# The opening of a two-layer encoder in a new written order, with the shift carried as a column

## The chip, the cores and the metric

The kernel runs on one core of a Trainium2 chip. The metric is the device time of one execution in microseconds. A core has TensorE (PE, matrix products), VectorE (DVE), ScalarE (ACT), GpSimd (POOL) and SyncE (SP, which here issues the DMAs). Each engine takes its instructions in one order and waits on semaphores for the others. Operands lie in SBUF, and TensorE writes its products to PSUM.

## The reference, cut to what matters

Two sequences, a prompt of 256 rows and a sample of 512 rows, go through a trunk of two layers. Layer 0 mixes with a two-way mLSTM of four heads, layer 1 with windowed attention, and each is followed by a convolutional feed-forward block. What the change touches is the front of layer 0:

```python
mod = silu(c) @ adaln_w[0] + adaln_b[0]          # c: one vector per sequence
sh1, sc1, g1, sh2, sc2, g2 = split(mod, 6)
h = rmsnorm(x, norm_g[0, 0]) * (1 + sc1) + sh1    # per sequence
proj = h @ w_in                                   # q, k, v, o and 16 gate columns
b = cumsum(log_sigmoid(f_gate)); m = running max of (i_gate - b) ...   # per head, both directions
```

Everything is float32. A product of two float32 matrices is built from three passes: each operand is split into a high half (`whi`, `hh`), rounded by ScalarE to the format that TensorE takes at full rate, and a low half (`wlo`, `hl`), the rest, by a subtraction on VectorE. Then high x high, high x low and low x high are added up in PSUM.

## The kernel before

Activations lie transposed: 1024 features as eight chunks (`KC`) of 128 partitions, and 768 columns, of which 0 to 255 are the prompt and 256 to 767 the sample. `RANGES` cuts them into the sample's two halves and the prompt (range 2). `hh` and `hl` hold the high and low halves of the normed input for all 768 columns.

*Norm.* `Norm` (L87 to L140) squares each chunk on ScalarE (L108), adds the squares up on GpSimd (L112, or on the engine given as `adds`), sums over partitions with products against a constant (two columns per 128 rows), takes the power -1/2 on GpSimd (L131), and broadcasts the result over the partitions by TensorE (`pr`). Then the `apply` function given to it scales the input. `stages()` is a generator: one call for the sums, one for the broadcast, one to apply.

*The opening* (L572 to L671) is written in an order by hand for TensorE, ScalarE and VectorE (`manual_schedule`). Its three items are the gates' weights and the two halves of head 0's query weights. It starts the sample's products before the adaLN shift is known. With x the normed input times its gain, (x + shift) W = xW + shift W, so the sample's item is accumulated from the unshifted input, and shift W is added as a bias: `bias(i, z)` multiplies the shift's two halves (`sh`, two columns) by each weight chunk into a spare corner of a PSUM bank, `biased(i)` copies the two columns out and adds them (L651, L652), and ScalarE adds the bias to the whole bank in place (L653). The prompt's items are computed from its shifted input. `shifted` then writes the shifted halves of the prompt and, between the items, of the sample, which all later products read. For the sample, every other chunk goes through ScalarE with a helper tile `hs` from which the shift is taken off again (L554, L556, L563).

The order on TensorE: sample range 0 and 1 items, shift products, prompt items interleaved with shift products. The `adaln` vectors of groups 1 (scale) and 0 (shift) are products of the conditioning vector with eight row tiles each (`vector`, L379 to L408).

*After it*, still in layer 0 but left to the planner, stand the gates' functions and scans. ScalarE computes the logarithm of the sigmoid (L765 to L767), VectorE sums it up along time in both directions (L773, L775), subtracts (L776), and takes running maxima (L779, L780). The maxima `M` go to DRAM (L784) and come back broadcast over partitions (L800). GpSimd adds the masks (L802). Then head 0: its key weights are split (L236 high, L237 low), four products of 24 passes give the keys (`gemmT`, two halves by two sequences), and `keep` evicts them in two halves (queries times 1/16, L239 and L240; keys unscaled, L236 and L237). Six tiles of values follow (`gemmN`, 24 passes each). Scores, exponentials of the masks (L864 to L868) and the weighted sums (L908 to L930) come next, and the same for heads 1 to 3.

*Filling.* Two generators, `adaln_v` (VectorE, layer 1, L472) and `adaln_g` (TensorE, layer 0), compute the rest of the adaLN vectors in small steps that the heads call. They fetch rows of 512 KB through the same five `raw` buffers as the weights. `issue_after` puts the first of `adaln_v` behind the last scan.

*The planner.* Outside the written stretches the order on each engine comes from the tile framework's list scheduler, which takes the instructions by priority (the order of the program) whenever its own model of time says that an engine is free. It can also put such instructions between those of a written stretch. SP and GpSimd are always ordered by it. PSUM has four banks under the name `ps` and four under `pa`; split weights have three buffers each for `whi` and `wlo`.

Of the kernel before, what the change touches and what calls it, by code (L numbers as in the profile page):

```python
# [145 lines left out]
class Net:  # L146
# [232 lines left out]
    def vector(self, pool, grp, rows):  # L379
# [3 lines left out]
        self.spare = ps = self.ps()  # L383
        for k in range(KC):
            for g in range(4):
                self.mm(
                    ps[32 * g : 32 * g + 32, :256], self.silc[:, k, :], rows[k][:, g * 256 : (g + 1) * 256],
                    k == 0, k == KC - 1,
                )
# [130 lines left out]

    def scaled(self, x, pr, rng):
# [4 lines left out]
    def unshifted(self, x, pr, rng):  # L526

        nc = self.nc
        c0, c1, q = rng
        for c in range(KC + 1):  # L530
            if c < KC:
                if pr is not None:
                    nc.vector.tensor_tensor(x(c), x(c), pr, ALU.mult)
                nc.scalar.activation(self.hh[:, c, c0:c1], x(c), AF.Copy, scale=self.gain[0][0][:, c, q : q + 1])
            if c:
                nc.vector.scalar_tensor_tensor(  # L536
                    self.hl[:, c - 1, c0:c1], x(c - 1), self.gain[0][0][:, c - 1, q : q + 1],
                    self.hh[:, c - 1, c0:c1].bitcast(F32), ALU.mult, ALU.subtract,
                )
        return ()  # L540

    def shifted(self, pool, xt, rng, less=None):

# [4 lines left out]
        sub = [None] * KC  # L548
        for c in range(KC + 1):
            if c < KC:  # L550
                gain, shift = self.gain[0][0][:, c, q : q + 1], self.mod[0][:, c, q : q + 1]
                hi = self.hh[:, c, c0:c1]
                if less is not None and c % 2:
                    nc.scalar.activation(hi, x(c), AF.Identity, bias=shift, scale=gain)  # L554
                    sub[c] = pool.tile([P, c1 - c0], F32, tag="E", name=self.nm("hs"), bufs=2)
                    nc.scalar.activation(sub[c], hi.bitcast(F32), AF.Identity, bias=less[:, c : c + 1])  # L556
                else:
                    nc.vector.tensor_scalar(x(c), x(c), gain, shift, ALU.mult, ALU.add)
                    nc.scalar.copy(hi, x(c))
            if c:  # L560
                hi, lo = self.hh[:, c - 1, c0:c1], self.hl[:, c - 1, c0:c1]
                if sub[c - 1] is not None:
                    self.behind_opening = nc.vector.scalar_tensor_tensor(  # L563
# [1166 lines left out]
```

## Time and profile before

| | us |
|---|---|
| median of 3 runs | 1902.51 |
| lowest, highest | 1899.25, 1902.64 |
| span of the profiled execution | 1900.1 |
| median less that span | 2.4 |
| TensorE busy in it | 1812.0 (95%) |
| VectorE, ScalarE, GpSimd busy | 1413.8, 920.9, 491.0 |
| mean granted TensorE clock | 0.983 |

The profiled execution's own time is its span with whatever lies before the first and after the last instruction. Only the span is recorded for it, and the runs' times are near it. Lines from the trace read: start, length, engine, line of the kernel, operation, output `<-` inputs, partitions x elements, how many; in brackets the idle time of the engine before it and what ended that. In a table of stretches each engine has its busy microseconds and its count of instructions; `PEclk` is the share of full speed that TensorE was granted. In a list of waits the numbers are the total, the count and the longest. In a list of groups they are the total busy time and the mean nanoseconds of one.

### The profile page before, as it was taken

How to read it: one execution, taken by the hardware profiler on the slowest of the kernel's cores; microseconds unless marked ns; L12 is line 12 of the kernel's file. 1: busy time of each engine (PE TensorE's matmuls, PEld its weight loads, DVE VectorE, ACT ScalarE, POOL GpSimd, SP SyncE). 2: the span in 40 equal slices, each digit the busy share in tenths (PEclk: the TensorE clock that was granted, in tenths of full speed). 3: DMA queues.
4: the chain of work that ended last, by engine and by line, in shares of the span. 5: the costliest groups of instructions: out<-in, count | busy, mean ns of one | idle time of the engine just before them, and what ended most of it. 6: DMA issues, size and time to landing. Idle time of an engine off the chain costs nothing.

```text
span 1900.1 us, 29288 instructions
## 1 busy us (share of the span) xinstructions
PE 1812.0 (95%) x11354; PEld 1672.5 (88%) x11354; DVE 1413.8 (74%) x2310; ACT 920.9 (48%) x1849; POOL 491.0 (26%) x395
## 2 busy tenths in 40 slices
PE   7889999999999999999999999989989999999997
PEld 5787887888998999999999988879979999999996
DVE  4664776687589877777777768875998777777777
ACT  4633434343456444444444466773564444444443
POOL 3001000022013433333332303330133333333322
PEclk9888999999999999999999999999999999999998
DMA  8243655456412222222222321212222222222211
GB/s 321 66 141 113 210 166 165 153 167 199 144 55 89 67 67 67 67 67 67 67 67 79 112 81 48 84 58 90 78 78 77 68 67 67 67 67 67 67 34 67
DMA packets 64246, 184.49 MB, mean 97 GB/s; under 512 B 6167, under 2 KB 23831, under 8 KB 64108
## 3 DMA queue, kind: packets, MB, share of 16 engines
q1 hardware_dynamic: 64108, 182.63, 29.6%
q8 instruction: 89, 1.46, 0.3%
q14 instruction: 49, 0.40, 0.1%
HBM read 176.17 MB, written 6.43 MB: 96 GB/s over the span
## 4 chain that ended last, share of the span: by engine, by line
PE 76%; DVE 11%; issue 5%; ACT 4%; DMA 2%; POOL 2%; SPq 0%; POOLq 0%; ACTq 0%; DVEq 0%
PE pa L230 23%; PE ps L230 23%; PE ps L1252 10%; PE ps L1253 9%; PE ps L1254 9%; DVE wlo L237 2%; DMA bt<-brow 1%; DVE slab L690 1%; ACT t L1078 1%; DVE t L1069 1%; POOL nt L112 1%; DVE slab L1479 1%; DVE zl L1210 1%; DVE slab L1478 0%; DVE slab L237 0%
## 5 line engine op out<-in xcount | busy, mean ns | idle before, releaser
L236 ACT CAST whi<-raw 128x1024 fp32r<-128x1024 f32 x237 | 248.7, 1049 | 401.1 <-PE pa L230 200.3
L237 DVE TENSOR_TENSOR wlo<-raw,whi 128x1024 fp32r<-128x1024 f32 x237 | 330.7, 1395 | 113.5 <-ACT whi L236 112.8
L230 PE MATMUL pa<-slab,whi 128*128 128x256 f32 (+1 forms) x1472 | 344.8, 331 | 4.4 <-DVE slab L690 4.2
L230 PEld LDWEIGHTS pa<-slab,whi 128*128 128x128 f32 x1472 | 250.9, 188 | 31.4 <-DVE slab L690 5.8
L690 DVE SCALAR_TENSOR_TENSOR slab<-pa,mod,slab 128x256 f32<-128x256 f32 (+1 forms) x368 | 207.8, 592 | 67.5 <-PE pa L230 66.9
L230 PE MATMUL ps<-zh,whi 128*128 128x256 f32 (+2 forms) x688 | 233.6, 340 | 4.4 <-ACT whi L236 2.6
L230 PE MATMUL pa<-slab,wlo 128*128 128x256 f32 (+1 forms) x736 | 234.0, 330 | 0.0
L230 PE MATMUL ps<-zh,wlo 128*128 128x256 f32 (+2 forms) x688 | 228.6, 335 | 4.3 <-DVE wlo L237 4.3
L230 PE MATMUL ps<-zl,whi 128*128 128x256 f32 (+2 forms) x688 | 229.0, 334 | 1.6 <-DVE zl L536 0.9
L1252 PE MATMUL ps<-zh,whi 128*128 128x384 f32 x504 | 171.2, 340 | 14.3 <-ACT ps L1307 13.1
L1253 PE MATMUL ps<-zl,whi 128*128 128x384 f32 x504 | 169.8, 337 | 1.7 <-DVE zl L1210 1.7
L1254 PE MATMUL ps<-zh,wlo 128*128 128x384 f32 x504 | 169.0, 335 | 0.0
L230 PEld LDWEIGHTS pa<-slab,wlo 128*128 128x128 f32 x736 | 138.3, 188 | 13.0 <-DVE wlo L237 0.9
L230 PEld LDWEIGHTS ps<-zh,whi 128*128 128x128 f32 x688 | 132.7, 193 | 18.0 <-ACT whi L236 3.2
L230 PEld LDWEIGHTS ps<-zh,wlo 128*128 128x128 f32 x688 | 132.4, 192 | 15.1 <-DVE wlo L237 5.1
L230 PEld LDWEIGHTS ps<-zl,whi 128*128 128x128 f32 x688 | 132.5, 193 | 11.2 <-DVE zl L536 1.3
L1505 POOL TENSOR_TENSOR slab<-slab 128x772 f32<-128x772 f32 x44 | 83.3, 1893 | 206.7 <-DVE slab L1479 193.9
L1283 POOL TENSOR_TENSOR raw<-raw,raw 128x512 f32<-128x512 f32 x40 | 52.1, 1303 | 294.1 <-DVE wlo L237 244.1
L1478 DVE SCALAR_TENSOR_TENSOR slab<-slab,cstt,slab 128x771 f32<-128x771 f32 x88 | 105.3, 1199 | 26.9 <-ACT slab L1476 26.9
L1479 DVE SCALAR_TENSOR_TENSOR slab<-slab,cstt,slab 128x771 f32<-128x771 f32 x88 | 119.7, 1360 | 0.8
L472 DVE SCALAR_TENSOR_TENSOR ada<-raw,silc,ada 128x1024 f32<-128x1024 f32 x84 | 114.0, 1387 | 6.5 <-DMA raw<-in_adaln_w_dram 6.3
L1252 PEld LDWEIGHTS ps<-zh,whi 128*128 128x128 f32 x504 | 94.7, 188 | 22.2 <-ACT ps L1307 18.2
(309 smaller groups left out, 4182.4 us busy)
## 6 DMA issues: line engine op xcount, KB each, us to landing
raw<-in_w_dram SPq DMA_DIRECT2D x208, 512.0 KB, 3.7
raw<-in_adaln_w_dram SPq DMA_DIRECT2D x84, 512.0 KB, 4.4
slab<-in_x_dram SPq DMA_DIRECT2D x12, 512.0 KB, 7.6
slab<-in_adaln_w_dram SPq DMA_DIRECT2D x12, 512.0 KB, 10.9
slab<-mrows SPq DMA_DIRECT2D x8, 384.0 KB, 5.7
xs<-slab SPq DMA_DIRECT2D x6, 512.0 KB, 2.9
bt<-brow SPq DMA_DIRECT2D x16, 192.0 KB, 3.2
slab<-xs SPq DMA_DIRECT2D x6, 512.0 KB, 6.7
```

Source lines behind the costliest of these rows:

```text
L230: self.last_mm = self.nc.tensor.matmul(out, lhsT, rhs, start=start, stop=stop)
L236: nc.scalar.copy(hi, src)
L237: return nc.vector.tensor_tensor(lo, src, hi.bitcast(F32), ALU.subtract)
L472: stt(acc[:, s], row, w, acc[:, s], ALU.mult, ALU.add)
L690: self.nc.vector.scalar_tensor_tensor(x, o, self.mod[l][:, gc + c, q : q + 1], x, ALU.mult, ALU.add)
L1252: mm(o, wh[:, k], hi[k], start=start and k == 0, stop=False, skip_group_check=True)
L1253: mm(o, wh[:, k], lo[k], start=False, stop=False, skip_group_check=True)
L1254: mm(o, wl[:, k], hi[k], start=False, stop=k == 3, skip_group_check=True)
L1283: tt(q[0], q[2], q[0], ALU.subtract)
L1478: stt(y[:, 1:], u[:, :-1], w(0), y[:, 1:], ALU.mult, ALU.add)
L1479: stt(y[:, :-1], u[:, 1:], w(2), y[:, :-1], ALU.mult, ALU.add)
L1505: nc.gpsimd.tensor_tensor(y, y, yrow[:, j], ALU.mult)
```

## The change

The stretch written by hand is longer: it now reaches over the gates' functions, the scans and the first keys. Part by part:

- The shift's products as separate two-column products are gone. Column 256 of `hh` and `hl` (the first of the sample) is overwritten with the sample's shift once the unshifted sample has been read, and the prompt's operand is two columns longer (`c1 += 2 * q`, 258). Column 256 of the prompt's item is then shift x W for the sample. `bb` and `bg` take it from there.
- The gates and the queries of the sample are evicted with that bias in one step each, instead of an addition in the PSUM bank and an eviction. In head 0 the factor 1/16 moves from the queries to the keys (`key`).
- The prompt's norm multiplies by the gain together with the norm (`gained`), and range 1 does the same in `unshifted`. Range 0 is multiplied by its gain afterwards by eight operations of VectorE. `shifted` then only adds: high on ScalarE with a bias, low on VectorE, and the helper tile goes.
- Range 1's sums of squares are added up on VectorE instead of GpSimd.
- The prompt's norm stages stand after chunks 4 and 5 instead of 2 and 5, and the shift's adaLN rows are taken in another order.
- The sample's shift runs after all prompt items, between the queries. The keys' weights are loaded and split in the opening, the four key products are written behind the prompt's items (prompt first), and their evictions stand before the gates' functions (prompt), between sums and maxima, and between the maxima (sample).

```diff
     def vector(self, pool, grp, rows, order=tuple(range(KC))):
...
+    def unshifted(self, x, pr, rng):
+        nc = self.nc
+        c0, c1, q = rng
+        gain = lambda c: self.gain[0][0][:, c, q : q + 1]
+        for c in range(KC + 1):
+            if c < KC:
+                if pr is not None:
+                    nc.vector.scalar_tensor_tensor(x(c), x(c), gain(c), pr, ALU.mult, ALU.mult)
+                    nc.scalar.copy(self.hh[:, c, c0:c1], x(c))
+                else:
+                    nc.scalar.activation(self.hh[:, c, c0:c1], x(c), AF.Copy, scale=gain(c))
...
+    def gained(self, x, pr, rng):
+        q = rng[2]
+        for c in range(KC):
+            self.nc.vector.scalar_tensor_tensor(
+                x(c), x(c), self.gain[0][0][:, c, q : q + 1], pr, ALU.mult, ALU.mult
+            )
         return ()
-    def shifted(self, pool, xt, rng, less=None):
+    def shifted(self, xt, rng):
...
+                nc.scalar.activation(self.hh[:, c, c0:c1], x(c), AF.Identity, bias=shift(c))
             if c:
...
+                nc.vector.scalar_tensor_tensor(lo, x(c - 1), shift(c - 1), hi.bitcast(F32), ALU.add, ALU.subtract)
             yield
-    def opening(self, pool, xt, rows, raws, consume):
+    def opening(self, pool, xt, rows, raws, gates, qt, kt):
...
+            Norm(self, xt, r, (self.scaled, self.unshifted, self.gained)[i], (2, 2, 0)[i], adds=(None, nc.vector)[i == 1])
...
+            c1 += 2 * q
...
+        for c in range(KC):
+            nc.vector.tensor_scalar(norms[0].x(c), norms[0].x(c), self.gain[0][0][:, c, 0:1], None, ALU.mult)
         item(2, 0, range(5))
...
+        vec = self.vector(pool, 0, rows[1], (0, 2, 3, 4, 5, 6, 7, 1))
...
         for k in range(KC):
             for i in range(3):
                 item(i, 1, (k,))
-            if k in (2, 5):
+            if k == 4:
                 stage(2)
             if k == 5:
+                stage(2)
                 self.step(vec, KC + 1)
             if k == 6:
                 self.step(vec)
+                self.fp_copy_split(self.hh[:, :, edge], self.hl[:, :, edge], self.mod[0][:, 0:KC, 0])
+        for _ in self.shifted(xt, PROMPT):
             pass
-        pb = lambda i: self.spare[:, 256 + 2 * i : 258 + 2 * i]
-        def bias(i, z):
-            for h in range(2):
-                self.mm(pb(i), ws[i][h][:, z], sh[:, z], z + h == 0, z + h == KC)
...
         for i in range(3):
+            item(i, 2)
+        sample = self.shifted(xt, SAMPLE)
...
+        wk = [weights()]
...
+        def query(i):
+            nc.vector.tensor_copy(bb[:, i - 1 : i], bank[i, 1][:, edge : edge + 1])
+            hi, lo = (qt[:, z, i - 1, a0:a1] for z in range(2))
+            nc.scalar.activation(hi, bank[i, 0], AF.Identity, bias=bb[:, i - 1 : i])
+            nc.vector.scalar_tensor_tensor(lo, bank[i, 0], bb[:, i - 1 : i], hi.bitcast(F32), ALU.add, ALU.subtract)
+            self.fp_copy_split(qt[:, 0, i - 1, b0:b1], qt[:, 1, i - 1, b0:b1], bank[i, 1][:, : b1 - b0])
...
+        query(1)
+        wk.append(weights())
+        self.step(sample, 4)
+        query(2)
+        self.step(sample, 5)
+        ks = {}
+        for q in (1, 0):
+            for c in range(2):
+                ks[c, q] = self.gemmT(wk[c], q)
+        key(0, 1)
+        key(1, 1)
+        yield
+        key(0, 0)
+        yield
+        key(1, 0)
+        yield
...
         with self.tc.manual_schedule(engines={eng.PE, eng.Activation, eng.DVE}):
-            self.opening(pool, xt, rows, raws, [gates, keep(qt0, 0, 0), keep(qt0, 0, 1)])
+            opening = self.opening(pool, xt, rows, raws, (gi, gf), *qk0)
+            next(opening)
+            nc.scalar.preload_act_table_set("natural_log_exp_and_others")
...
+            for s0, s1 in SEQS:
+                scan(F[0:4, s0:s1], lf[0:4, s0:s1], z[0:4, s0:s1], 0.0, ALU.add, ALU.add)
...
+            next(opening)
+            nc.vector.tensor_tensor(a, gi, F, ALU.subtract)
+            for s0, s1 in SEQS:
+                b = slice(s0, s1)
+                scan(M[0:4, b], a[0:4, b], z[0:4, b], 0.0, ALU.max, ALU.add)
+                if s0 == SEQS[0][0]:
+                    next(opening)
```

152 lines of the change are left out of this document (57 added, 95 removed).

## The prediction

> **What bounds the kernel now.** I read the share of busy time first, then the busy time by stretch, then TensorE's waits, then the timeline around them.
>
> ```profile
> PE 1812.0 (95%) x11354; PEld 1672.5 (88%) x11354; DVE 1413.8 (74%) x2310; ACT 920.9 (48%) x1849; POOL 491.0 (26%) x395
> ```
>
> ```profile
> core 0: us, PE busy (x) PEld busy (x) DVE busy (x) ACT busy (x) POOL busy (x), PEclk, DMA share, GB/s
> ...
> 51.50:74.00 22.50, 18.95 (x122) 18.74 (x121) 14.65 (x35) 15.41 (x26) 0.00 (x0) 0.70 0.09 27
> 74.00:90.70 16.70, 16.70 (x98) 14.58 (x96) 11.58 (x15) 11.60 (x17) 0.00 (x0) 1.00 0.18 60
> 90.70:119.80 29.10, 20.17 (x147) 19.87 (x146) 19.62 (x26) 5.52 (x9) 4.62 (x2) 0.82 0.41 130
> ...
> 170.00:1900.00 1730.00, 1672.89 (x10387) 1550.42 (x10385) 1315.44 (x2114) 840.84 (x1674) 461.27 (x364) 0.99 0.28 90
> ```
>
> TensorE bounds the run. After 170 us it is busy 1672.9 of 1730 us at a clock of 0.99, so time won before 170 us should pass to the end. The weak part is where the diff works: from 51.5 to 119.8 us TensorE idles 12.5 us and runs 15.9 us more at half clock:
>
> ```profile
> PE ps L230 <- DVE slab L237: 8.9, 1, 8.9
> PE pa L926 <- ACT hs L922: 4.1, 1, 4.1
> PE ps L230 <- DVE bb L652: 3.6, 1, 3.6
> ```
>
> ```profile
> 57.40:67.80 10.40, 10.40 (x49) 10.40 (x50) 4.20 (x8) 7.21 (x11) 0.00 (x0) 0.50 0.01 2
> ...
> 99.80:105.30 5.50, 5.50 (x25) 5.50 (x26) 5.16 (x5) 0.00 (x0) 3.25 (x2) 0.50 0.52 186
> ```
>
> The 3.6 us wait is for the copy of the shift's product out of PSUM (L651, L652). That copy stands on VectorE behind the whole prompt's shift, and the next shift product writes the same bank. The 8.9 us wait is for the keys' low halves (L237), which stand behind the gates' scans. A half-rate stretch follows each. The words "half rate" mean a start every 0.213 us for a product of 256 columns, against 0.12 us.
>
> **Step 1, up to the last product of the second sample range (51.49 us).**
>
> ```profile
> 31.42 1.50 PE L230 MATMUL pa<-inv,nt 128*128 128x2 f32 x12 [1.19 <-POOL nt L112]
> ```
>
> ```profile
> 32.96 0.16 DVE L130 TENSOR_SCALAR nr<-pa 128x2 f32<-128x2 f32 x1 [3.79 <-PE pa L230]
> ...
> 37.49 0.48 DVE L536 SCALAR_TENSOR_TENSOR zl<-slab,gain,zh 128x256 fp32r<-128x256 f32 x1 [0.24 <-ACT zh L534]
> 37.89 0.42 DVE L533 TENSOR_TENSOR slab<-slab,pa 128x256 f32<-128x256 f32 x1
> 38.22 0.48 DVE L536 SCALAR_TENSOR_TENSOR zl<-slab,gain,zh 128x256 fp32r<-128x256 f32 x1
> ```
>
> The second range's sums of squares move from GpSimd to VectorE. Five adds of 0.42 us (taking L533's 128x256 form) fill the 3.79 us in which VectorE was idle, and TensorE's wait of 1.19 us for GpSimd goes. The eight new multiplications of the first range by its gain (one source, 128x256, 0.41 us each busy) stand on VectorE while the norm's power and broadcast run; at worst they hold the second range's scaling by about 1 us. In that scaling one pair per chunk stays one pair: the products' operand and its low half start 0.73 us apart (37.49 to 38.22), and TensorE needs 9 x 0.12 = 1.07 us for a chunk, so it hides. The prompt's norm steps now stand one chunk apart (after chunks 4 and 5), and a sum, a GpSimd power and a broadcast need about 1.4 us in a chunk of 1.07: minus 0.3 us. With 1.19 - 0.3 the step gains 0.9 us. Bounds: -0.5 (the multiplications on the path) and 2.5 (the half-rate microseconds around 34 us go as well).
>
> **Step 2, the prompt's products (51.49 to 74.00 us).** Removed are 48 products of two columns (three items, eight chunks, a high and a low half) and the bank's wait; the shift rides as column 256 of the prompt's operand, 258 columns instead of 256.
>
> ```profile
> L567 DVE TENSOR_TENSOR zl<-slab,zh 128x256 fp32r<-128x256 f32 x8 | 3.4, 422 | 0.3
> L558 DVE TENSOR_SCALAR slab<-slab,gain,mod 128x256 f32<-128x256 f32 x8 | 3.2, 409 | 0.0
> ...
> L554 ACT ACTIVATE zh<-slab,mod,gain 128x512 fp32r<-128x512 f32 x3 | 2.4, 812 | 0.0
> ```
>
> TensorE now has nothing between the last sample product and the prompt's first: high half on ScalarE, low half on VectorE, about 0.4 us each, part of it under the last nine products, so I take a stall of 0.5 us. The first 24 products go at the pace of eight low halves (0.41 us against 3 x 0.12 on TensorE): 3.3 us. The other 48 take 48 x 0.12 = 5.8 us. The two added columns are nothing: products of 258 columns with 30 in 3.74 us further down the trace are 0.125 us apart.
>
> ```profile
> 146.65 3.74 PE L230 MATMUL pa<-slab,PT 128*128 128x258 f32 x30
> ```
>
> Sum 9.6 us against 22.5: a gain of **12.9 us**. Bounds: 13.8 without stall, 6.2 if all 72 run at half rate (72 x 0.093 = 6.7 us more). This ends at 51.5 - 0.9 + 9.6 = 60.2 us.
>
> **Step 3, the first keys (74.00 to 90.70 us).** The same 96 products, now written by hand behind the prompt's: 16.7 us at clock 1.00, gain 0. Cover: their weights' splits need a buffer freed by the first and second item's prompt products (54 and 57 us) plus 1.04 + 1.22 us, and the second is due at 63; the sample's shift starts when the prompt's products have read column 256, and its eight 0.75 to 0.81 us halves end near 68 us, while the keys of the sample start at 66 and take 0.68 us a chunk. If that cover fails, each microsecond of it counts in full; I allow 2. Keys end at 76.9 us instead of 90.7.
>
> **Step 4, the first values (90.70 to 119.8 us).** Here the 8.9 us wait and 5.5 us of half rate stand.
>
> ```profile
> 79.40 1.28 ACT L766 ACT_TABLE_LOAD   x1
> ...
> 82.86 0.94 ACT L767 ACTIVATE slab<-slab,ones 36x768 f32<-36x768 f32 x1
> ```
>
> ```profile
> 83.83 0.95 DVE L770 TENSOR_TENSOR slab<-slab 36x768 f32<-36x768 f32 x1 [4.60 <-ACT slab L767]
> 84.88 1.21 DVE L773 TENSOR_TENSOR_SCAN slab<-slab,slab 4x512 f32<-4x512 f32 x1
> ...
> 88.74 1.23 DVE L237 TENSOR_TENSOR wlo<-raw,whi 128x1024 fp32r<-128x1024 f32 x1
> ...
> 94.00 0.68 DVE L780 TENSOR_TENSOR_SCAN slab<-slab 4x256 f32<-4x256 f32 x1
> ...
> 99.34 0.40 DVE L237 TENSOR_TENSOR slab<-ps,slab 128x256 fp32r<-128x256 f32 x1
> ```
>
> The new order puts the keys' evictions before, between and inside the scans. ScalarE's queue from 50.2 us: eight highs 3.3, two weight splits 2.1, gates and their two bias columns 2.7, two queries 2.0, the sample's eight highs 6.5, two small keys 0.7, about 1 of waiting for TensorE, then one table load instead of two and three gate functions (1.28 + 0.84 + 0.85 + 0.94): the logarithm ends near 72.4 us, not 83.8. The scans with their subtractions and two key halves of 0.67 end at 72.4 + 0.95 + 3.8 + 0.67 + 0.94 + 1.22 + 0.67 + 2.57 = 83.2 us. The values' banks are then free in time: the third tile starts at 76.9 + 5.8 = 82.7 and its bank is read out at 77.8. What is late next is the values' own weights: their two splits are outside the written order, so the planner puts their low halves (1.23 us each) into a gap of VectorE's order, as at 88.74 between scans, or behind the last scan. I take 2 us of stall for it: one half fits ahead of the scans, the other in the gap where a scan waits for the subtraction (near 79 us, needed at 78.4 us). Bounds 0 and 9.9 (the first rival). The products take 144 x 0.12 = 17.3 us, so the stretch shrinks from 29.1 to 19.3: **9.8 us**.
>
> **Step 5, what comes after.**
>
> ```profile
> 102.05 4.62 POOL L802 TENSOR_TENSOR slab<-slab,kct 128x768 f32<-128x768 f32 x2 [58.18 <-DMA slab<-mrows]
> ```
>
> ```profile
> 120.78 0.40 ACT L865 ACTIVATE E<-slab,aT 128x128 f32<-128x128 f32 x1 [0.59 <-DVE aT L792]
> ```
>
> From the last scan (94.68) to the masks (106.67) is 12.0 us of DMAs, SP's queue and GpSimd. With scans ending at 83.2 to 85.7 the masks come at 95 to 98 us, and the values end at 96.2: the exponentials start about when they are wanted, and scores and the next head's projections cover a microsecond. Nothing is taken off. SP's and GpSimd's lists keep their transfers; the scans' row store leaves with the scans.
>
> Sum: 0.9 + 12.9 + 0 + 9.8 = **23.6 us**. The profiled execution's span is 1900.1, which lies among the runs (1899.25 to 1902.64) and 2.4 below their median: 1900.1 - 23.6 + 2.4 = **1878.9 us**, own range 1873 to 1885.
>
> **The rivals.**
>
> *The values' splits fall behind the last scan.* For it: VectorE's written order has something ready nearly all the time from 72 to 83 us. Then the first half comes at 84.4 instead of 76.9, 7.5 us of stall, and a half-rate stretch like that of 99.8 us (25 products, 25 x 0.093 = 2.4): 9.9 instead of 2. Against: before, one was placed between scans. Time 1886.8.
>
> *The clock stays low through the prompt's products.* For it: the half-rate stretch at 57.4 us follows a wait of only 3.6 us, and it lasted 10.4 us with two-column products among the others. Against: those products go, and the stall shrinks to 0.5 us. Price 6.7 us: 1885.6. [...]
>
> *More than the sum.* After the first head's values VectorE stands behind its adaLN row, TensorE waits 4.1 us (L926) and the clock falls:
>
> ```profile
> 150.00:170.00 20.00, 15.26 (x95) 13.11 (x94) 9.99 (x25) 9.47 (x32) 6.38 (x5) 0.74 0.42 107
> ```
>
> ```profile
> 151.37 2.48 DVE L472 SCALAR_TENSOR_TENSOR ada<-raw,silc,ada 128x1024 f32<-128x1024 f32 x2 [0.37 <-DMA raw<-in_adaln_w_dram]
> ```
>
> The wait and 20 x 0.26 = 5.2 us of clock make 9.3 us. A new order of the planner there can lose this place: 1869.6.
>
> *Slower.* The same place repeated: adaLN multiplications stand in VectorE's queue ahead of the denominators, each waiting for its row of 512 KB. If the earlier start leaves the rows late in three of the four heads, three times 9.3 = 27.9 us are lost; from the third on the gain of 23.6 is gone: 1906.8. Against: the rows' loads are released by VectorE's own multiplications and the weight splits, which all come earlier too, and the DMA share there is under half.
>
> **How the numbers follow.** Forecast 0.52, splits behind the scans 0.24, low clock 0.08, more than the sum 0.09, slower 0.07. The range 1868 to 1893 holds the first four with 6 us of reordering above the dearest, and leaves out the last. A change under 0.2% (3.8 us) can't be told from none; faster than 1898.7 are the first four nearly whole: 0.90 faster, 0.03 same, 0.07 slower.
>
> **What would show it.** Step 1: no GpSimd wait near 31 us. Step 2: no two-column products, no wait on a bias copy, prompt's products within 10 us from about 51. Step 3: keys done near 77 us. Step 4: the 8.9 us wait gone or down to 2, the last scan before 86 us. Step 5: exponentials from about 97 us; after it stretches as long as before. I am wrong if the values still end after 105 us, or if they end early and the time past 170 us grows.

## The result, and the profile after

The changed kernel takes **1881.96 us** (median of 4 runs, 1881.14 to 1885.06), and the kernel before on the same chip 1901.64 us. The ratio is 0.9897, with a 95% interval from 0.9884 to 0.9909: faster by 1.03%, near the forecast of 1878.9 us and inside its range. The profiled execution took 1885.06 us, with a span of 1883.3; the other three spans lie between 1879.2 and 1880.3. So two traces of the changed kernel are read here, this one and that of a second run with a span of 1880.2.

First the busy time by engine of the changed kernel, then its busy time by stretch. The columns of the stretches are those of the prediction: busy time of TensorE, its weight loads, VectorE, ScalarE and GpSimd, then the granted clock, the DMA share and the rate.

```profile
PE 1799.4 (96%) x11306; PEld 1659.1 (88%) x11306; DVE 1412.1 (75%) x2306; ACT 912.2 (48%) x1841; POOL 488.7 (26%) x390
```

```profile
37.20:52.70 15.50, 15.43 (x147) 13.37 (x147) 9.26 (x28) 3.68 (x11) 0.71 (x1) 0.89 0.43 156
52.70:62.20 9.50, 9.36 (x75) 9.16 (x74) 5.90 (x13) 8.41 (x18) 0.00 (x0) 1.00 0.23 76
62.20:78.80 16.60, 16.60 (x98) 14.74 (x97) 15.02 (x22) 12.57 (x19) 0.00 (x0) 1.00 0.32 95
78.80:96.50 17.70, 17.63 (x145) 17.28 (x143) 15.37 (x22) 3.20 (x7) 4.27 (x2) 1.00 0.45 139
96.50:125.00 28.50, 28.50 (x180) 22.45 (x180) 21.47 (x32) 14.22 (x36) 0.24 (x1) 1.00 0.51 169
125.00:143.00 18.00, 11.01 (x80) 9.20 (x79) 9.43 (x23) 8.44 (x27) 4.59 (x3) 0.84 0.42 130
```

The prompt's products (52.7 to 62.2), the first keys (to 78.8) and the first values (to 96.5) now run without idle time and at full clock, a start every 0.12 us for 256 columns: 43.8 us, where the kernel before took 68.2 (51.5 to 119.7). (What the rounding buys shows in the kernel before: products of halves with 512 columns, L230 `ps<-zh,whi`, take 0.41 us on average, its two of unrounded float32, L230 `pa<-oh,rb`, 0.59 us.) The stretch from 125 to 143 us still has 7 us of idle time and a clock of 0.84. TensorE's list of waits up to 170 us, the lines that bear on the prediction:

```profile
PE pa L949 <- ACT hs L945: 5.4, 1, 5.4
PE ps L230 <- ACT zh L531: 1.7, 1, 1.7
PE pa L230 <- ACT hs L936: 1.6, 1, 1.6
PE pa L230 <- DVE nt L112: 0.8, 1, 0.8
```

The waits of 8.9 and 3.6 us are gone, and the one of 1.19 us on GpSimd's sums has become one on VectorE's, 0.8 us here and 0.2 in the second run. There is a new one of 1.7 us (L531), and the wait in front of the first head's transposes has grown from 4.1 to 5.4 us (L949, before L926) with 1.6 us more ahead of it.

How far the changed kernel is ahead can be read from landmarks that every trace has: the six small transposes behind the first values (36x36), the first transposes of the first head's output (L926, now L949), and ScalarE's loads of its function table. From the timelines of the kernel before, of the changed kernel, and of the second run of the changed kernel:

```profile
119.71 0.56 PE L791 MATMUL pa<-kct,slab 36*128 36x36 f32 x6
...
158.19 0.69 PE L926 MATMUL pa<-kct,hs 128*128 128x128 f32 x2 [4.11 <-ACT hs L922]
...
392.39 1.28 ACT L942 ACT_TABLE_LOAD   x1
...
585.38 1.28 ACT L1503 ACT_TABLE_LOAD   x1
...
1129.10 1.28 ACT L1081 ACT_TABLE_LOAD   x1
```

```profile
96.52 0.56 PE L818 MATMUL pa<-kct,slab 36*128 36x36 f32 x6
...
369.41 1.28 ACT L965 ACT_TABLE_LOAD   x1
...
561.07 1.28 ACT L1526 ACT_TABLE_LOAD   x1
...
1110.81 1.28 ACT L1104 ACT_TABLE_LOAD   x1
```

```profile
51.47 0.38 PE L230 MATMUL pa<-zh,whi 128*128 128x258 f32 x1
...
95.24 0.56 PE L818 MATMUL pa<-kct,slab 36*128 36x36 f32 x6
...
136.93 0.69 PE L949 MATMUL pa<-kct,hs 128*128 128x128 f32 x2 [5.47 <-ACT hs L945]
...
368.76 1.28 ACT L965 ACT_TABLE_LOAD   x1
...
561.91 1.28 ACT L1526 ACT_TABLE_LOAD   x1
...
1110.26 1.28 ACT L1104 ACT_TABLE_LOAD   x1
```

The lead is 23.2 us at the end of the values (second run 24.5), 21.3 in the second run at the transposes, 23.0 (23.6) near 390 us of the kernel before, 24.3 (23.5) near 585 us, 18.3 (18.8) near 1129 us, and 16.8 (19.9) at the end of the span. So the opening won what the sum said. The first head gave back 3 us of it, which were won again by 390 us; behind 585 us the lead shrinks for good, to 4.6 to 6.4 us below what it was at the end of the values. Why is the first question for the experiments; the second is the new wait of 1.7 us.

### The profile page after: what moved, and what is told of

Same layout as the page of the kernel before. It is cut to its first block, busy times and chain, and to the rows that moved or that the text cites. A ratio compares the mean times of both kernels' runs of the same rounds, so it can differ in the third digit from the quotient of the medians.

```text
span 1883.3 us, 29169 instructions
## 1 busy us (share of the span) xinstructions
PE 1799.4 (96%) x11306; PEld 1659.1 (88%) x11306; DVE 1412.1 (75%) x2306; ACT 912.2 (48%) x1841; POOL 488.7 (26%) x390
## 5 line engine op out<-in xcount | busy, mean ns | idle before, releaser
L237 DVE TENSOR_TENSOR wlo<-raw,whi 128x1024 fp32r<-128x1024 f32 x237 | 331.1, 1397 | 113.9 <-ACT whi L236 108.5
L230 PE MATMUL pa<-slab,whi 128*128 128x256 f32 (+1 forms) x1472 | 347.3, 333 | 4.8 <-DVE slab L719 4.6
L230 PEld LDWEIGHTS pa<-slab,whi 128*128 128x128 f32 x1472 | 253.0, 190 | 31.8 <-DVE slab L719 6.3
L230 PE MATMUL ps<-zh,whi 128*128 128x256 f32 (+2 forms) x688 | 232.5, 339 | 6.1 <-ACT whi L236 2.6
L230 PE MATMUL pa<-slab,wlo 128*128 128x256 f32 (+1 forms) x736 | 235.2, 331 | 0.0
L230 PE MATMUL ps<-zh,wlo 128*128 128x256 f32 (+2 forms) x688 | 227.0, 332 | 3.8 <-DVE wlo L237 3.8
L230 PE MATMUL ps<-zl,whi 128*128 128x256 f32 (+2 forms) x688 | 227.9, 332 | 1.4 <-DVE zl L539 0.9
L1275 PE MATMUL ps<-zh,whi 128*128 128x384 f32 x504 | 171.2, 340 | 16.7 <-ACT ps L1330 15.2
L230 PEld LDWEIGHTS pa<-slab,wlo 128*128 128x128 f32 x736 | 139.5, 190 | 13.0 <-DVE wlo L237 0.9
L230 PEld LDWEIGHTS ps<-zh,whi 128*128 128x128 f32 x688 | 131.0, 191 | 20.0 <-issue 3.5
L230 PEld LDWEIGHTS ps<-zh,wlo 128*128 128x128 f32 x688 | 131.2, 191 | 14.8 <-DVE wlo L237 4.8
L230 PEld LDWEIGHTS ps<-zl,whi 128*128 128x128 f32 x688 | 131.3, 191 | 10.4 <-DVE zl L539 1.1
```

The source lines that it names most:

```text
L230: self.last_mm = self.nc.tensor.matmul(out, lhsT, rhs, start=start, stop=stop)
L237: return nc.vector.tensor_tensor(lo, src, hi.bitcast(F32), ALU.subtract)
L1275: mm(o, wh[:, k], hi[k], start=start and k == 0, stop=False, skip_group_check=True)
```

## The experiments

All experiments start from the changed kernel. Times are medians, and their differences are taken from the 1882.68 us of its second run. The ratios are to the kernel before on the same chip, which gave 1901.88 to 1902.11 us on the three chips used. Each experiment has one trace. The start of the opening itself varies by one to two us from run to run (the first product of the sample starts between 21.5 and 23.2 us), so edits behind it are judged by the distance from the prompt's first product to the end of the values, 95.24 - 51.47 = 43.8 us in the second run of the changed kernel.

### The changed kernel again

> The changed kernel once more, as the measure for its neighbours on the same chip. Every theory expects a time near 1881 us, some 20 us under the kernel before. Its trace also says whether the last 4 to 5 us by which the profiled run of 1885.1 us lay above the other runs' spans belong to the kernel: if they do, the stretch near 1040 to 1060 us shows the granted clock near 0.83 again; if they come and go, its clock stands near 1.00 there.

1882.68 us (1878.51 to 1883.66, 4 runs), ratio 0.9896 (0.9879 to 0.9912), span 1880.2. The place asked about is where the attention layer begins. These are 35 us there, in the kernel before, in the first and in the second trace of the changed kernel:

```profile
1050.00:1085.00 35.00, 32.59 (x268) 31.56 (x267) 28.17 (x63) 19.64 (x43) 13.87 (x17) 1.00 0.36 121
```

```profile
1030.00:1065.00 35.00, 31.75 (x234) 30.53 (x232) 25.05 (x55) 17.39 (x41) 15.60 (x17) 0.90 0.35 119
```

```profile
1029.00:1064.00 35.00, 32.16 (x236) 30.94 (x234) 25.05 (x56) 17.65 (x40) 15.26 (x17) 0.90 0.34 114
```

In both traces of the changed kernel the clock is 0.90, and some 33 products fewer are started in the 35 us. So the 3.5 us of clock lost there did not come and go between these two runs, and the idea that they set the first trace apart fell. Of the 3.1 us between the two spans, 2.6 lie behind the table load near 1110 us, from which it takes 772.5 us to the end in the first trace and 769.9 in the second.

### The gain's multiplications later

```diff
-        for c in range(KC):
-            nc.vector.tensor_scalar(norms[0].x(c), norms[0].x(c), self.gain[0][0][:, c, 0:1], None, ALU.mult)
         item(2, 0, range(5))
         stage(1)
...
+        gain0(range(5))
         item(2, 0, range(5, KC))
...
             if k == 4:
                 stage(2)
+                gain0(range(5, KC))
```

> The eight multiplications of the first sample range by the gain go from in front of the second range's scaling to VectorE's idle places behind it (five in the 2.52 us before the prompt's mean, three in the 1.59 us behind it). Theory: these eight operations (4.11 us on VectorE) are what the second range waits for. Then its scaling starts near 33.9 us instead of 36.20, TensorE's wait of 1.69 us at 37.2 is gone, the prompt's first product starts at about 51.0 us instead of 52.70, and the time falls by 1.0 to 1.7 us below the changed kernel. Rival: the row of the shift (its last sum near 52.0 us) sets the start of the prompt's products, and the wait at 37.2 only moves there; then the first product starts at 52.2 us or later and the time falls by 0 to 0.5 us.

1881.37 us (1876.42 to 1885.15, 5 runs), ratio 0.9890 (0.9873 to 0.9907). The times overlap with those of the changed kernel; the traces tell more. In the changed kernel VectorE's timeline and TensorE's next wait were:

```profile
32.17 4.11 DVE L624 TENSOR_SCALAR slab<-slab,gain 128x256 f32<-128x256 f32 x8
36.20 0.86 DVE L530 SCALAR_TENSOR_TENSOR slab<-slab,gain,pa 128x256 f32<-128x256 f32 x2
```

```profile
37.16 0.39 PE L230 MATMUL ps<-zh,whi 128*128 128x256 f32 x1 [1.69 <-ACT zh L531]
```

With the edit:

```profile
34.27 0.87 DVE L530 SCALAR_TENSOR_TENSOR slab<-slab,gain,pa 128x256 f32<-128x256 f32 x2 [2.18 <-PE pa L230]
...
40.66 1.40 DVE L628 TENSOR_SCALAR slab<-slab,gain 128x256 f32<-128x256 f32 x5
```

```profile
49.70 0.39 PE L230 MATMUL pa<-zh,whi 128*128 128x258 f32 x1
```

The range's scaling starts 1.9 us earlier, the wait of 1.7 us is gone, and the prompt's first product starts at 49.70 us against 51.47 in the second run of the changed kernel, 1.8 us earlier. Of these, 0.4 us stood already at the sample's first product (21.48 against 21.91), so the edit is worth 1.3 us there. The theory of the wait holds, and its rival (the shift's row would take over) falls; the fall of the whole time that it expected is not shown.

The row at 40.66 shows something else: five multiplications take 1.40 us, 0.28 each, where the same eight took 4.11, 0.51 each, at 32.17 us. At 32 us GpSimd is at work (29.5 to 35.9 us, adds of squares but for 0.8 us), at 40.7 it stands idle. The transfers differ too, with a DMA share of 1.03 from 30 to 40 us in the changed kernel against 0.43 from 40 to 50 us with the edit, but another pair of rows speaks against them as the cause. The same subtraction of a weight split, in the kernel before beside GpSimd's adds and in the changed kernel with GpSimd idle, has a DMA share of 1.01 and 1.02:

```profile
27.45 1.71 DVE L237 TENSOR_TENSOR wlo<-raw,whi 128x1024 fp32r<-128x1024 f32 x1 [0.79 <-ACT whi L236]
```

```profile
28.08 1.22 DVE L237 TENSOR_TENSOR wlo<-raw,whi 128x1024 fp32r<-128x1024 f32 x1
```

In both pairs the row beside a busy GpSimd is the longer one, 0.51 us against 0.28 and 1.71 us against 1.22. Why VectorE is slower there, no run shows.

### The shift's column alone

```diff
-        opening = self.opening(pool, xt, rows, raws, (gi, gf), *qk0)
-        next(opening)
...
+        self.opening(pool, xt, rows, raws, (gi, gf), qt0)
```

The opening ends with the second query here. The gates' functions, the scans and the keys stand outside the written order, in the text of the kernel before. This kernel leaves out the factor 1/16 in head 0; its keys are evicted unscaled, as in the kernel before.

> The shift as a column, the moved products, the gain and the new order up to the queries' evictions stay; the keys, the gates' functions and the scans are left to the planner, as in the kernel before. Theory (steps 2 and 4 add up, each for itself): the prompt's products take 9.5 us as in the changed kernel, and the first values are late again, 29 us with a wait of 8 to 9 us in them, so the last scan ends 9 to 10 us later after the opening than in the changed kernel; time 9 to 11.5 us above the changed kernel and 10 to 12 below the kernel before. Rival: once the opening no longer spills its products into the keys, the planner finds room for the values' weights by itself; the wait falls below 3 us and the time is within 2 us of the changed kernel.

1888.91 us (1884.05 to 1895.15, 6 runs), ratio 0.9936 (0.9917 to 0.9955). From TensorE's waits and its timeline:

```profile
PE ps L230 <- DVE slab L237: 10.8, 1, 10.8
```

```profile
52.87 0.39 PE L230 MATMUL pa<-zh,whi 128*128 128x258 f32 x1
...
110.15 0.56 PE L794 MATMUL pa<-kct,slab 36*128 36x36 f32 x6
...
147.88 0.69 PE L929 MATMUL pa<-kct,hs 128*128 128x128 f32 x2 [3.28 <-ACT hs L925]
```

From the prompt's first product to the end of the values it takes 57.3 us, 13.5 more than the changed kernel. The prompt's products still take 9.5 us, so steps 2 and 4 are separate, as the theory says. The time rises by 6.2 us, less than its 9 to 11.5: of the 13.5 us, 4.0 come back up to the first head's transposes, which follow 37.7 us behind the end of the values instead of 41.7, and more further on. VectorE's timeline shows what the written order does, and it is not earlier scans:

```profile
83.06 0.68 DVE L783 TENSOR_TENSOR_SCAN slab<-slab 4x256 f32<-4x256 f32 x1
83.77 1.42 DVE L470 TENSOR_SCALAR ada<-raw,silc 128x1024 f32<-128x1024 f32 x2
...
89.53 0.40 DVE L237 TENSOR_TENSOR slab<-ps,slab 128x256 fp32r<-128x256 f32 x1
```

The last scan ends at 83.7 us, earlier than in the first trace of the changed kernel (85.45 us). But the planner puts the second layer's first rows (L470) and other work behind the scans, and only then the keys' evictions.

### Key evictions behind the scans, and ahead of them

```diff
-            next(opening)
...
-                if s0 == SEQS[0][0]:
-                    next(opening)
...
+            for _ in opening:
+                pass
```

> The evictions of the sample's two key products go from among the scans to behind the last of them; nothing else changes. Theory: their accumulators are what the values' third and fourth products need, so these wait from about 83 us until the last scan is done and one eviction behind it (85.5 to 86.5 us); the first values end 3 to 6 us later than 96.5 us, more by up to 3.5 us if TensorE's wait is followed by a stretch at half clock, and the time rises by 3 to 8 us over the changed kernel. Rival: the place of the evictions is free, because the accumulators in rotation cover it; values end within 0.5 us of 96.5 and the time is the same within 2 us.

1885.27 us (1879.69 to 1887.26, 4 runs), ratio 0.9917 (0.9901 to 0.9934), with a profiled span of 1877.8. The theory of 3 to 6 us falls: the distance is 44.0 us against 43.8, with one wait of 0.3 us.

```profile
52.40 0.38 PE L230 MATMUL pa<-zh,whi 128*128 128x258 f32 x1
...
96.43 0.56 PE L817 MATMUL pa<-kct,slab 36*128 36x36 f32 x6
```

Scans without evictions among them end sooner (at 83.96 us against 85.45), and two evictions right behind the last (83.99 to 85.28 us) are in time. What matters is that they stand ahead of the rows, not that they stand among the scans. The median is 2.6 us higher, but the intervals of the two ratios overlap and the profiled span is lower; I take no loss from it.

The other way round, all four key evictions ahead of the gates' functions:

```diff
-            next(opening)
+            for _ in opening:
+                pass
             nc.scalar.preload_act_table_set("natural_log_exp_and_others")
...
```

> All four key evictions go ahead of the gates' functions and scans, so that the logarithm's chain waits for the last key product (78.8 us). Theory: the last scan then ends 6 to 9 us later than 85.45 us, GpSimd's masks 6 to 9 us later than 96.75 us, and the first exponentials, which start at 100.3 us in the changed kernel, wait for the masks and start at 103 to 106 us; the products of the first head's tiles wait with them, and the time rises by 2 to 5 us. Rival: the exponentials are not what the first head waits for (TensorE has the second head's keys to go on with), and the time is the same within 1 us although they start later.

1892.02 us (1889.23 to 1893.57, 4 runs), ratio 0.9948 (0.9933 to 0.9962), 9.3 us above the changed kernel. From TensorE's timeline:

```profile
53.74 0.38 PE L230 MATMUL pa<-zh,whi 128*128 128x258 f32 x1
...
99.55 0.58 PE L230 MATMUL ps<-whi,zh 128*128 128x256 f32 x1 [8.00 <-DVE slab L237]
...
107.49 0.56 PE L816 MATMUL pa<-kct,slab 36*128 36x36 f32 x6
```

53.8 us instead of 43.8. The last scan ends at 94.4 us, as late as in the kernel before. But my reason was wrong: the exponentials start 1.6 us behind the end of the values (3.9 in the changed kernel) and hold nothing. What stands still is TensorE, 8.0 us, for the evictions of the first values (L237), which are queued behind the scans and the rows. So the order pays for two things, evictions of keys and of values, and the scans have to be over before the values need theirs.

### Why the prompt's products ran at half clock before

Four runs take apart the 22.5 us of step 2. In the first, `two(i, k)` multiplies the two weight halves of a chunk by two columns, into a bank that nothing reads:

```diff
-        for i in range(3):
-            item(i, 2)
...
+        for k in range(KC):
+            two(0, k)
+        for k in range(KC):
+            item(0, 2, (k,))
+            two(1, k)
+        item(1, 2)
+        for k in range(KC):
+            two(2, k)
+        item(2, 2)
```

> The 48 products of two columns stand among the prompt's products again, in the order that they had in the kernel before, into a bank that nothing reads; the shift stays a column, and there is no copy of a bias to wait for. Theory A (the wait of 3.55 us made the half clock in the kernel before): the prompt's products take 9.5 us and 48 times 0.11 us, together 14 to 15.5 us, all at full clock, and the time rises by 4.5 to 6 us. Theory B (the two-column products themselves bring the clock down): the granted clock falls to 0.5 to 0.8 in them, the stretch takes 18 to 22 us, and the time rises by 8.5 to 12.5 us.

1888.50 us (1887.50 to 1890.91, 4 runs), ratio 0.9932 (0.9918 to 0.9947), 5.8 us above the changed kernel. By stretch:

```profile
54.00:70.00 16.00, 16.00 (x137) 16.00 (x137) 9.67 (x17) 12.29 (x24) 0.00 (x0) 1.00 0.22 67
```

Full clock all the way: theory A. The values end at 101.19 us against 95.24, of which 1.3 us stood already at the sample's first product (23.21 against 21.91): the 48 products cost 4.7 us, 0.1 each. Now a wait without these products:

```diff
+        for c in range(6):
+            x = xt[c // 4][:, c % 4, 0:512]
+            nc.vector.tensor_scalar(x, x, 1.0, None, ALU.mult)
         for _ in self.shifted(xt, PROMPT):
```

> Six multiplications by one, on 512 columns each, stand on VectorE in front of the prompt's shift; nothing else changes. They hold TensorE for some 4 to 6 us ahead of the prompt's products, somewhat longer than the 3.55 us for which the kernel before held it among them. Theory A: a wait of this length alone brings a stretch at half clock of about 10 us as in the kernel before, so that the prompt's products take 9.5 + 5 us at least, and the time rises by the wait and 5 us more, 9 to 11 us. Theory B: the half clock lasts some 3.4 us, as in the stretches around 1036 to 1056 us of the changed kernel, and costs 1.7 us; the time rises by 5.5 to 8 us. Theory C: the wait costs itself alone, 4 to 6 us, with a clock of 1.00 in the products.

1884.95 us (1882.74 to 1888.32, 4 runs), ratio 0.9913 (0.9899 to 0.9928). The multiplications took 0.35 us each, so the wait was shorter than meant, 0.5 + 1.15 us. A stretch with the clock at 0.79 follows:

```profile
54.00:62.00 8.00, 7.09 (x46) 7.09 (x47) 4.85 (x11) 4.66 (x12) 0.00 (x0) 0.79 0.01 2
```

8 x 0.21 = 1.7 us of clock are lost, 3.4 us at half clock: theory B in its length, behind a wait of half the length. Up to the end of the values the two cost 2.9 us (0.5 ahead of the prompt's first product, and 46.1 us behind it instead of 43.8); the time rises by 2.3. With twelve multiplications, then:

```diff
+        for c in range(12):
+            x = xt[c // 4 % 2][:, c % 4, 0:512]
+            nc.vector.tensor_scalar(x, x, 1.0, None, ALU.mult)
```

> Twelve multiplications by one in front of the prompt's shift, no two-column products: TensorE waits some 3.6 to 3.9 us ahead of the prompt's second product, as long as in the kernel before (3.55 us). Theory: the half clock behind a wait without two-column products lasts 3.4 us however long the wait is (it lasted 3.4 us behind 1.7 us); the values end 4.2 + 2.1 = 6.3 us later than in the changed kernel. Rival: a wait of 3.55 us alone brings the half clock of 10 us or more; the values end 9 to 11 us later.

1885.39 us (1883.18 to 1887.37, 4 runs), ratio 0.9905 (0.9888 to 0.9921).

```profile
54.00:66.00 12.00, 9.33 (x54) 9.04 (x55) 7.35 (x19) 6.86 (x15) 0.00 (x0) 0.72 0.04 7
```

A wait of 3.2 + 0.3 us comes with 12 x 0.28 = 3.4 us of clock lost, 6.7 us at half clock, a little of it inside the wait itself. The theory's fixed 3.4 us falls, and so does the rival's 10. From the sample's first product to the end of the values it takes 80.6 us, 5.8 more than in the first trace of the changed kernel, whose sample products ran as long; of these 5.8 us the time shows 2.7. At last both together, the two-column products as above and seventeen multiplications:

```diff
+        for c in range(17):
+            x = xt[c // 4 % 2][:, c % 4, 0:512]
+            nc.vector.tensor_scalar(x, x, 1.0, None, ALU.mult)
...
+        for k in range(KC):
+            two(0, k)
```

> The 48 products of two columns among the prompt's products, as in the run with them alone, and 17 multiplications by one (0.35 us each) on VectorE in front of the prompt's shift, so that TensorE waits some 3.5 us behind the first sixteen of them. Theory: the half clock of the kernel before needs both, the wait to begin it and the two-column products, in which TensorE's array stands idle much of the time, to keep it; then the clock is near 0.5 for 10 us or more behind the wait, as in the kernel before (0.77, 0.50, 0.50, 0.52 in four stretches of 4 us), and the values end 5 to 7 us later than the wait and the 5.95 us of these products alone make them. Rival: the wait alone sets the half clock, and the two-column products add only their 5.95 us to the run with the longer wait alone.

1895.93 us (1894.32 to 1899.64, 6 runs), ratio 0.9969 (0.9957 to 0.9981), 13.3 us above the changed kernel. TensorE waited 4.2 us. By stretch:

```profile
54.00:74.00 20.00, 15.81 (x81) 15.49 (x82) 9.77 (x25) 6.86 (x15) 0.00 (x0) 0.57 0.11 34
```

20 x 0.43 = 8.6 us of clock, 17 us at half clock, of which some 3 us fall inside the wait. The same products without a wait ran at full clock, and a wait of 3.5 us without them brought 6.7 us at half clock: the long stretch needed both. The times say so too. The products alone cost 5.8 us and the wait alone 2.7, 8.5 in sum, and both together 13.3. The extra of some 5 us is at the lower end of the 5 to 7 that the theory gave for the end of the values. The waits of the two runs were not quite equal (4.2 and 3.5 us), and how much half clock a wait brings varies between the two traces of the changed kernel by one stretch of 3.4 us (38.3 to 41.7 us, see the last section), so the 10 us between 6.7 and 17 are good to some 3 us. That TensorE's array stands idle much of the time in the two-column products was an estimate: in this trace they start 0.11 us apart at full clock (53.9 to 55.4 us), hardly less than products of 256 columns with 0.12 us. No run shows the activity itself, nor why the clock stays low behind a wait.

### The rows of the adaLN vectors later

```diff
                     if t % 2 == 0:
-                        self.step(self.fill)
+                        self.step(self.fill, 1 if h else 0)
...
-                        if q <= c or h > 1:
+                        if h:
                             self.step(self.fill)
```

> Three of the second layer's rows, with their transfers of 512 KB and their six VectorE operations of 1.24 us, go from the first head's values to the second head's queries and keys. Theory: between 97 and 138 us the changed kernel gives back 2 us because weights and rows come late (ScalarE's splits wait 2.45 and 4.11 us on weight transfers at 121.4 and 127.5 us) and the rows stand in front of the first head's exponentials' products and denominators; without them TensorE's waits of 1.6 and 5.4 us near 129 and 138 us shrink by 2 us or more together, and the time falls by 1 to 3 us below the changed kernel. Rival: the transfers are the limit of the whole stretch and the rows collide with the second head's weights instead, so the loss only moves; time within 0.5 us of the changed kernel or above it.

1881.35 us (1880.03 to 1882.77, 4 runs), ratio 0.9893 (0.9878 to 0.9908): not to be told from the changed kernel. ScalarE's waits for weights between the end of the values and the first transposes, in the kernel before and in the changed kernel, show what the theory started from:

```profile
ACT whi L236 <- DMA raw<-in_w_dram: 4.0, 2, 2.1
```

```profile
ACT whi L236 <- DMA raw<-in_w_dram: 11.4, 4, 4.1
```

With the edit they shrink to 4.1 us, and the wait for the denominators is down to 0.6 us. Another has come:

```profile
PE ps L230 <- DMA raw<-in_adaln_w_dram: 5.2, 1, 5.2
```

The rows of the first layer, which TensorE takes (`adaln_g`), are late in its place. The loss moved, as the rival had it. The last two runs moved those, with the gain's multiplications later too, the first without and the second with the edit just shown:

```diff
-                self.step(self.fillp, 2)
+                self.step(self.fillp, (0, 3, 3, 2)[h])
```

> The gain's multiplications stand later as in the run with this change alone, and besides the four row steps of the first layer at the first head's denominators (two ahead of each sequence, each with a 512 KB transfer and four products on TensorE) are spread over the next two heads (three ahead of each sequence there). Theory: the first head's denominators are late because rows stand in the queue of transfers in front of the second head's weights (splits that wait 2.45 and 4.11 us at 121 and 127 us in the changed kernel); with four rows fewer the waits of 1.3 and 5.4 us that the run with the later gain kept shrink by 3 us or more together, and the time falls by 3 to 6 us below the changed kernel. Rival: as with the three rows of the second layer moved, another row or weight takes their place; 1 to 2 us, what the gain's place alone is worth.

> As the run before it, and the three row steps of the second layer go from the first head's values to the second head's queries and keys as well. Theory: the wait of 5.2 us for a row of the first layer at 134.7 us, which took the place of the wait for the denominators when these three rows alone were moved, is gone; no wait above 3 us is left between 95 and 150 us, and the time falls by 4 to 8 us below the changed kernel. Rival: the rows crowd into the second head, whose weights then come late; a new wait of some us stands between 150 and 250 us and the time is within 2 us of the changed kernel with the gain's later place.

The first gave 1879.41 us (1878.80 to 1880.68, 4 runs), ratio 0.9878 (0.9863 to 0.9893); the second 1883.41 us (1882.38 to 1884.63, 4 runs), ratio 0.9899 (0.9884 to 0.9913). In the first the transposes start at 132.8 us instead of 136.9, 1.4 us of that ahead of the prompt's first product, but at the next table load the lead is gone (371.04 against 368.76 us). TensorE does not wait longer on the way there (6.9 against 6.5 us idle, though now for weight splits and a row): the 32 products of the moved rows stand there, and the clock is 0.97 instead of 0.99. That it ends lower comes from further on: the clock is 1.00 instead of 0.98 up to the table load near 560 us, and 1.00 instead of 0.90 in the 35 us of the attention's start. So it has the lowest median of all, but its interval overlaps that of the changed kernel, and the edit's own mechanism does not explain the difference. In the second, the wait of 5.2 us for a row is gone, but the one in front of the transposes (4.4 us) stayed, so its theory falls.

## Why the prediction was right, and where not

**Step 1** said plus 0.9 us. From the sample's first product to the end of the sample's products it took 29.9 us before (21.56 to 51.49), and 31.0 and 29.6 in the two traces after (21.67 to 52.70, 21.91 to 51.47): minus 1.1 and plus 0.4. The two differ by 1.5 us of clock, 0.89 in the first's stretch above. The failing term is the eight multiplications that "at worst hold the second range's scaling by about 1 us", at 0.41 us each. They take 0.51 each beside GpSimd's adds, 4.11 us together, and stand in one block in front of the scaling. Put elsewhere, they gave back 1.3 us, which makes plus 1.7 of the plus 0.4. The exchange of GpSimd's sum for VectorE's brought what was forecast, nearly: the product of the sums starts 8.9 us behind the sample's first in both traces, and started 9.9 us behind it before. The wait in front of that product shows less, because it also depends on how long the products ahead of it run. In the second trace they have a half-clock stretch, as in the kernel before, and the wait is 0.2 us:

```profile
30.81 1.50 PE L230 MATMUL pa<-inv,nt 128*128 128x2 f32 x12 [0.18 <-DVE nt L112]
```

**Step 2** said 12.9 us, and it was 13.0 (22.5 to 9.5). What it could not see is the make-up: 3.6 us of wait, 4.7 of two-column products, and the rest, 4.8, is clock. The rival of a clock that stays low did not come: in the changed kernel's two traces and in the run with the two-column products alone, these products run without a wait and at full clock. The runs put its price, for a wait alone, at 1.7 to 3.4 us of clock and not 6.7.

**Step 3** said 16.7 us and no gain, and it is 16.6.

**Step 4** said 9.8 us and gave 11.4 (29.1 to 17.7). The 2 us of stall for the values' weights did not come: their low halves stand at 65.4 and 74.5 us on VectorE, ahead of the scans. The last scan ends at 85.45 us, inside the 83.2 to 85.7 given. The rival that had these splits behind the scans is out. The reason given, that the evictions stand among the scans, was half right: behind the last scan they do as well, as long as the rows stay behind them.

**Step 5** took nothing off, and here the sum was too good. The timelines of GpSimd and ScalarE in the changed kernel:

```profile
92.23 4.52 POOL L829 TENSOR_TENSOR slab<-slab,kct 128x768 f32<-128x768 f32 x2 [46.27 <-DMA slab<-mrows]
```

```profile
100.31 0.40 ACT L888 ACTIVATE E<-slab,aT 128x128 f32<-128x128 f32 x1 [1.38 <-DVE aT L819]
```

The masks end at 96.75 us, inside 95 to 98; the exponentials start at 100.3, not 97, behind a weight split that waited for its transfer. From the end of the values to the transposes the first head takes 41.7 us instead of 38.5: 3.2 us go because the values end 23 us earlier and the second head's weights and rows do not. That is the mechanism of the slower rival at a third of its price for one head, and in one head instead of three. By the table load near 390 us it is made up for, because the kernel before has stretches of low clock (0.97 from the transposes to there) that are missing after (0.99), such as this one:

```profile
330.00:340.00 10.00, 9.85 (x52) 8.11 (x52) 9.57 (x15) 2.34 (x6) 0.71 (x1) 0.83 0.71 227
```

The loss that stays was in no step: 4.6 to 6.0 us between the table loads near 585 and 1129 us, 3.5 us of it the clock at the attention's start, behind waits that both kernels have. The prediction had named a growing time past 170 us as a sign that it is wrong. This sign came, in small: behind the first head's transposes the kernel before took 1741.9 us and the changed kernel 1745.1 and 1743.3.

So the sum of 23.6 met the 23.2 to 24.5 us at the end of the values partly by luck, through a step 1 that was too good by 0.5 to 2 us and a step 4 too careful by 1.6. The 3 us by which the time came out above 1878.9 were lost behind 585 us, in code that the change does not touch, and how much is lost there differs by some 4 us between nearly equal programs (last section).

## What to carry to other kernels

Price a VectorE operation by a row with the same neighbours: beside a busy GpSimd the same multiplication took 0.51 us instead of 0.28, and a block of cheap operations ahead of one that TensorE needs has its price: the eight of 4.11 us cost 1.3 us. When a written order ends a wait, look for what is queued behind the wait's engine and put the evictions ahead of the filling work; that counted here (10 and 13.5 us at the end of the values, 9.3 and 6.2 us in the whole time), not their exact place among the scans. Look at what an earlier finish will meet: transfers that are not earlier held the first head back by 3 of 24 us, though that was made up for further on.

## What the runs showed of the hardware that was not expected

A wait of 1.7 us of TensorE was followed by 3.4 us at half clock, and one of 3.5 us by 6.7. The same wait need not bring the same: behind the wait of 1.7 us at L531 the clock was 0.64 from 37.2 to 41.0 us in the first trace of the changed kernel, and 1.00 from 37.4 to 41.0 us in the second. The 35 us at the attention's start, taken 79.1 us ahead of the table load behind them in every trace, ran at 1.00 in the kernel before and in four experiments, at 0.95 in five, and at 0.90 in the two traces of the changed kernel and in two experiments, with nearly the same program there.

From the table load near 585 us to that near 1129 us the kernel before took 543.7 us, and the thirteen traces of the changed kernel and its variants 545.5 to 549.7. They follow that clock: 545.5 to 546.9 us where it was 1.00, 546.0 to 548.1 where it was 0.95, and 548.2 to 549.7 where it was 0.90. So most of the lead lost there is half clock that comes and goes between nearly equal programs, and differences of 2 to 4 us between kernels that share a long rest can arise far from the edit. Why the kernel before is the lowest of all, by 1.8 us at least, is open.
